# The modulated input of the QKV projection: full-precision value on ScalarE, traced with priority, low-part products last

## The chip, the core and the metric

One NeuronCore of one Trainium2 chip runs the whole program. The metric is the device time of one execution in microseconds; the kernel before took 1095.94 us (median of 3 runs, 1095.34 to 1098.32). Its engines, by the names of the profile: PE (TensorE matmul), PEld (its weight loads), DVE (VectorE), ACT (ScalarE), POOL (GpSimd), SP (the queue that issues the large loads). Each engine works through a queue of its own, in an order fixed when the program is built.

## The reference, cut to what matters

One layer of an encoder trunk: 256 tokens, width 2048, float32. The input is modulated by a scale and a shift that come from a conditioning vector, projected to queries, keys and values, and goes through attention, a projection, a layer norm, a modulated MLP and a second layer norm.

```
c_act = silu(c)
mod = c_act @ mod_w + mod_b                  # (2048,) @ (2048, 12288)
sh_m, sc_m, g_m, sh_f, sc_f, g_f = split(mod, 6)
hmix = x * (1 + sc_m) + sh_m                 # 256 x 2048
proj = hmix @ w_qkv + b_qkv                  # 2048 x 3072
...                                          # rotary positions, windowed attention with a sink
x = layer_norm(alpha * x + (1 + g_m) * (o @ w_o + b_o))
hff = x * (1 + sc_f) + sh_f
x = layer_norm(alpha * x + (1 + g_f) * (relu(hff @ w1 + b1)**2 @ w2 + b2))
```

## The kernel before

**Products in two parts.** Each operand of a large matmul is split into a rounded high part (type float32r) and a low part, the difference between the full value and the high part. A product is three matmuls on PE (function `mm3`): high input by high weight (L498), high input by low weight (L499), low input by high weight (L500). A weight tile `raw` (128 x 2048 floats, 1 MB) is loaded by SP (L202) and cut in two halves; for each half ACT writes the high part `wh` (L247) and DVE the low part `wl` (L218). There are five buffers of `wh` and five of `wl`, and eight of `raw` at first; a `raw` buffer is free again when both of its halves have been through L218, or when its other user is done.

**The modulation.** The input's 2048 features are 16 slices of 128. They are handled in six groups, g = 0 to 5, of 1, 1, 2, 4, 4 and 4 slices. For each group the scale and shift are themselves a product of the conditioning vector with 2 MB to 8 MB of weights (`in_modm`), done from the same `raw` buffers: partly on PE (L307), partly on DVE (L343, L345), whose part PE adds in at the end (L307 reading `onesf`). ACT copies the sums to `mrow` (L361), PE transposes them (L377), DVE adds the bias (L383) and one (L384), which gives the columns `scm` and `shm`.

**The modulated input.** The function `modulated(g)` then makes, for each slice of 128 x 256, the high part `hh` on ACT (L519), the full value in place on DVE (L520), and the low part `hl` = full minus high on DVE (L521). Groups 0 to 2 and, by `tc.keep_in_program_order`, these three instructions of every group are held to the order in which they were written; other instructions are placed by the scheduler of the framework, by their place in the trace and its estimate of when they can run.

**The projection.** A weight tile of a group of four slices is one chunk: four slices by 512 of the 3072 columns, which is 24 matmuls of 128 x 512. The function `qkv(g, ch)` runs a chunk: for each pair of slices, for both halves of the tokens, the three matmuls of each slice. Group 3 has six chunks in a row; here they are called chunk 1 to 6 of group 3. Groups 4 and 5 have three chunks each in this stage; the rest of theirs comes between the attention's steps. Results collect in PSUM (five buffers `pa`, two to a chunk) and are added to SBUF by DVE (`evict`, L537), two instructions to a chunk. Chunk 6 of group 3 is not evicted: it goes on into the first chunk of group 4 in the same two buffers. A group's last chunk calls `modulated(g + 1)` in its middle.

**Around it.** SP issues a load as soon as a `raw` buffer is free, in a planned order in which the modulation's weights and the chunks alternate. A one-element square root on ACT (`warm`, L874) stands in the trace after the attention, before the first layer norm (L761).

Of the kernel before, what the change touches and what calls it, by code (L numbers as in the profile page):

```python
# [2 lines left out]

# [1 line left out]

# [6 lines left out]
F32 = mybir.dt.float32  # L12
F32R = mybir.dt.float32r
I32 = mybir.dt.int32
AF = mybir.ActivationFunctionType
OP = mybir.AluOpType
# [4 lines left out]
S = 256  # L21
NT = S // 128
# [26 lines left out]
def hybrid_kernel(ctx: ExitStack, tc: tile.TileContext, a, out: bass.AP):  # L49
    nc = tc.nc  # L50
    cst = ctx.enter_context(tc.tile_pool(name="cst", bufs=1))
    sml = ctx.enter_context(tc.tile_pool(name="sml", bufs=4))
# [15 lines left out]
    def g4b(dt=F32):  # L68
        if not more:
            early.close()  # L70
            more.append(ctx.enter_context(tc.tile_pool(name="gen2", bufs=2 * MORE)))
        return more[0].tile([128, 1024], dt, tag="g4b", name="g4b")

    def g4(dt=F32):
        return gen.tile([128, 1024], dt, tag="g4", name="g4")

    def f32(x):
        return x.bitcast(F32)
# [5 lines left out]
    modmb, modfb, lnT = (pack[:, 80 + 32 * n:112 + 32 * n].rearrange("p (n k) -> p n k", n=2) for n in range(3))  # L84
# [8 lines left out]
    eps = cst.tile([128, 1], F32, name="eps")  # L93
# [73 lines left out]
    def bias_all(src, b):  # L167

        for h in range(2):
            nc.gpsimd.dma_start(b[h], src[:, h * 1024:h * 1024 + 1024].partition_broadcast(128))  # L170
        return lambda c: b[c // 2][:, (c % 2) * 512:(c % 2) * 512 + 512]
# [108 lines left out]
    S = Stream()  # L280
# [84 lines left out]
    def columns(m, mb, dst, k0, nk):  # L365

        r = m.r
        pt = pst.tile([128, 512], F32, name="pt")
        if m.pairs:
            nc.tensor.matmul(pt[:, :2], r[:, :128], both, start=True, stop=True)  # L370
            nc.vector.scalar_tensor_tensor(dst[0][:, k0:k0 + 1], pt[:, 0:1], 1.0, mb[:, 0, k0:k0 + 1],
                                           op0=OP.add, op1=OP.add)
            nc.vector.tensor_add(dst[1][:, k0:k0 + 1], pt[:, 1:2], mb[:, 1, k0:k0 + 1])
            return
        nh = m.w // 128
        for h in range(nh):
            nc.tensor.transpose(pt[:, h * 128:(h + 1) * 128], r[:, h * 128:(h + 1) * 128], ident)  # L377
        v = pt[:, :nh * 128].rearrange("p (h j q) -> p j h q", h=nh, j=4)[:, :, :, 0]
        cols = slice(k0, k0 + nk)
        for n in range(2):  # L380
            d = dst[n][:, cols].rearrange("p (j h) -> p j h", j=2)
            b = mb[:, n, cols].rearrange("p (j h) -> p j h", j=2)
            nc.vector.tensor_tensor(d, v[:, 2 * n:2 * n + 2], b, op=OP.add)  # L383
        nc.vector.tensor_scalar_add(dst[0][:, cols], dst[0][:, cols], 1.0)  # L384
# [28 lines left out]
    scm = cst.tile([128, NK], F32, name="scm")  # L413
    shm = cst.tile([128, NK], F32, name="shm")
# [77 lines left out]
    acc, xts, held, xs = {}, {}, {}, [None] * 4  # L492
# [4 lines left out]
    def mm3(ps, xh, xl, wh, wl, start, stop):  # L497
        nc.tensor.matmul(ps, xh, wh, start=start, stop=False)  # L498
        nc.tensor.matmul(ps, xh, wl, start=False, stop=False)  # L499
        S.prev = nc.tensor.matmul(ps, xl, wh, start=False, stop=stop).ins  # L500
# [10 lines left out]

    def modulated(g):
        m, k0, nk = m_mix[g]
        columns(m, modmb, (scm, shm), k0, nk)
        hh, hl = g4(F32R), g4(F32R)
        for k in range(nk):
            s = slice(k * 256, k * 256 + 256)
            xt, sc, sh = xts.pop(k0 + k), scm[:, k0 + k:k0 + k + 1], shm[:, k0 + k:k0 + k + 1]
            tc.keep_in_program_order(nc.scalar.activation(hh[:, s], xt, AF.Identity, scale=sc, bias=sh))  # L519
            tc.keep_in_program_order(nc.vector.tensor_scalar(xt, xt, sc, sh, op0=OP.mult, op1=OP.add))  # L520
            tc.keep_in_program_order(nc.vector.tensor_sub(hl[:, s], xt, f32(hh[:, s])))  # L521
        held[g] = hh, hl

    half = {}
# [1 line left out]
    def evict(c, pss):  # L526

        new = c not in acc
        if new:
            acc[c] = g4()  # L530
        for t in range(NT):
            av = acc[c][:, t * 512:t * 512 + 512]
            if new:
                bq(pss[t], c)
                nc.scalar.copy(av, pss[t])
            else:
                nc.vector.tensor_add(av, av, pss[t])  # L537

    def banks():
        return [psa.tile([128, 512], F32, name="pa") for _ in range(NT)]  # L540
# [22 lines left out]
    def qkv(g, ch):  # L563

        _, k0, nk = m_mix[g]
        hh, hl = held[g]
        wh, wl = S.main()
        per = 4 // nk
        for ci in range(per):
            p = ch * per + ci  # L570
            c = CORD[p]
            go_on, held_back = c in half, ((g, ch), p) in CARRY
            pss = half.pop(c, None) or banks()
            for k2 in range(0, nk, 2):
                for t in range(NT):
                    for k in (k2, k2 + 1):
                        s = slice(k * 256 + t * 128, k * 256 + t * 128 + 128)
                        mm3(pss[t], hh[:, s], hl[:, s], wh(ci * nk + k), wl(ci * nk + k),
                            k == 0 and not go_on, k == nk - 1 and not held_back)
                S.done()  # L580
                if per == 1 and k2 == 0:
                    yield
            if held_back:
                half[c] = pss
            else:
                evict(c, pss)
            if per == 2 and ci == 0:
                yield

    def run(gen, mid=()):  # L590
        next(gen)
        for f in mid:
            f()
        for _ in gen:
            pass
# [63 lines left out]
    def pairs_T(src, n):  # L659

        out = g4()
        for pr in range(n // 2):
            pt = pst.tile([128, 512], F32, name="pt")
            for i in range(2):
                for t in range(NT):
                    x = t * 512 + (pr * 2 + i) * 128
                    nc.tensor.transpose(pt[:, i * 256 + t * 128:i * 256 + t * 128 + 128], src[:, x:x + 128], ident)
            nc.scalar.copy(out[:, pr * 512:pr * 512 + 512], pt)
        return out
# [100 lines left out]
    sc = []  # L770
# [53 lines left out]
    def mids(n):  # L824
        out = []
        if 0 < n <= 16:
            out.append(lambda: probs_T(n - 1))
        if n < 16:
            out.append(lambda: normalise(n))
        return out  # L830
# [3 lines left out]
    for n in range(21):  # L834
        j, i = n // 4, n % 4
        if n < 16:
            scores(n)
        for f in todo:
            f()
        todo = []  # L840
        if n == 1:
            S.deep = False
        if n == 5:
            assert all(h is raws for h in S.home[S.at:]), "an early buffer is still in use"
        if n + 1 < len(LATE):
            w = qkv(*LATE[n + 1])
        else:
            if n == 5:
                ys, bo = [g4b() for _ in range(4)], bias_all(a["bo"], [g4b(), g4b()])
            w = project((n - 5) // 4, (n - 5) % 4)  # L850
        mid = mids(n)
        if j < 3:
            if i == 0:
                turn = rope(j + 1, 1)
            if 0 < i < 3 or n and i == 0:
                mid.append(lambda: qA.__setitem__(j + 1, next(turn)))
            if i == 3:
                mid.append(lambda: qT.__setitem__(j + 1, pairs_T(qA[j + 1], 4)))
        run(w, mid)
        if n == 0:  # L860
            next(turn)
        if 0 < n <= 16 and n % 2 == 0:
            todo.append(values(n - 1))
        if n == 9:

            for c in range(4):
                xs[c] = g4()
                i = nc.gpsimd.dma_start(xs[c].rearrange("p (t n) -> p t n", t=NT), a["x"][:, :, 512 * c:512 * c + 512])
                tc.add_manual_dep(i.ins, S.prev.name, AFTER, reason="not sooner")
        if n == 12:  # L870
            g1 = gate(m_gm)
        if n == 16:
            warm = sml.tile([128, 1], F32, name="warm")
            nc.scalar.activation(warm, eps, AF.Sqrt)  # L874
            st = [sml.tile([128, 4, 6], F32, name=f"st{t}", bufs=2) for t in range(NT)]


# [77 lines left out]
    for n, (kg, fq) in enumerate(W1A):  # L955
# [3 lines left out]
        wh, wl = S.main()  # L959
        for fp in range(2):  # L960
# [3 lines left out]
            for fi in range(2):  # L964
                o = ps[:, fi * 256:fi * 256 + 256]
                for k in range(4):
                    w = (fp * 2 + fi) * 4 + k
                    hb = ff_in(4 * kg + k)
                    hh, hl = hb[:, :256], hb[:, 256:]
# [91 lines left out]
    for c in range(3):  # L1061
        pss = ff_out(blk, us, c)
# [6 lines left out]
    for t in range(NT):  # L1069
# [5 lines left out]
        for c in (1, 0, 2, 3):  # L1075
            z = part(xs, t, c)
            g, b = (gb[n][c // 2][:, (c % 2) * 512:(c % 2) * 512 + 512] for n in range(2))
# [98 lines left out]
```

## Time and profile before

| | |
|---|---|
| Runs of the kernel before | 1095.34, 1095.94, 1098.32 us |
| The profiled execution: its own time | 1100.0 us |
| Its span, first to last instruction | 1098.2 us |
| PE busy | 1067.6 us (97%) |
| DVE busy | 804.2 us (73%) |
| ACT busy | 522.0 us (48%) |
| Mean granted TensorE clock | 0.991 |

The profile counts an engine as busy while an instruction of its runs; PE's ends are modelled, so neighbouring matmuls overlap in the records. Idle time is put down to what ended it. Times inside the execution are counted in microseconds from the first instruction. The stage that the change touches lies between about 37 and 145 us.

### The profile page before, as it was taken

What the parts mean: (1) busy time and instruction counts of PE and PEld (TensorE: products, weight loads), DVE (VectorE), ACT (ScalarE), POOL (GpSimd) and SP (SyncE); (2) the same over time, 40 slices, a digit from 0 to 9 for tenths busy, and PEclk for the clock granted to TensorE, in tenths of its full rate; (3) what the DMA queues carried; (4) which work ended last, traced back from release to release, by engine and by line L of the source; (5) the groups of instructions that cost most, each with busy time, mean ns of one, the idle gap of its engine ahead of it and who ended that gap; (6) DMA issues with size and microseconds to landing.
All of it is one profiled execution on the core that took longest, in us unless ns stands there. A gap on an engine that the chain in (4) does not pass through costs nothing.

```text
span 1098.2 us, 15487 instructions
## 1 busy us (share of the span) xinstructions
PE 1067.6 (97%) x6098; PEld 863.1 (79%) x6098; DVE 804.2 (73%) x1162; ACT 522.0 (48%) x806; POOL 30.0 (3%) x54
## 2 busy tenths in 40 slices
PE   8889999998999999999999999999999999999995
PEld 6657677665677799988888888888888888888884
DVE  4597899978899877754588889756666557665676
ACT  5333346765673537643344543344453334544340
POOL 1000000001000000000000010001000000000001
PEclk9989999999999999999999999999999999999998
DMA  9999987789985996555578788866555555557511
GB/s 384 425 427 425 427 357 280 271 297 379 377 315 201 361 360 244 185 192 192 195 301 303 272 313 306 312 220 225 184 189 190 197 196 186 178 185 267 191 75 77
DMA packets 43337, 292.70 MB, mean 267 GB/s; under 512 B 5104, under 2 KB 5232, under 8 KB 9472
## 3 DMA queue, kind: packets, MB, share of 16 engines
q1 hardware_dynamic: 39312, 279.85, 66.9%
q0 software_dynamic: 3200, 10.50, 2.7%
q10 hardware_dynamic: 752, 1.35, 0.3%
q8 instruction: 48, 0.79, 0.3%
q14 instruction: 25, 0.20, 0.0%
HBM read 289.57 MB, written 2.11 MB: 266 GB/s over the span
## 4 chain that ended last, share of the span: by engine, by line
PE 86%; DVE 7%; DMA 4%; ACT 2%; issue 1%; DVEq 0%; ACTq 0%
PE pa L995 16%; PE pa L500 15%; PE pa L498 15%; PE pa L499 15%; PE pa L996 8%; PE pa L972 3%; PE pa L971 3%; PE pa L973 3%; PE pm L307 3%; DVE wl L218 2%; DMA raw<-in_modm 2%; DMA raw<-in_modf 1%; DVE g L345 1%; DMA raw<-in_wqkv 1%; PE pa L687 1%; PE pa L743 1%
## 5 line engine op out<-in xcount | busy, mean ns | idle before, releaser
L218 DVE TENSOR_TENSOR wl<-raw,wh 128x1024 fp32r<-128x1024 f32 x332 | 403.9, 1223 | 223.6 <-ACT wh L247 222.9
L247 ACT CAST wh<-raw 128x1024 fp32r<-128x1024 f32 x332 | 347.1, 1051 | 441.3 <-PE pa L500 228.6
L498 PE MATMUL pa<-wh,g 128*128 128x512 f32 x816 | 324.1, 398 | 5.1 <-ACT g L519 2.6
L500 PE MATMUL pa<-wh,g 128*128 128x512 f32 x816 | 318.9, 392 | 4.1 <-DVE g L521 3.0
L499 PE MATMUL pa<-wl,g 128*128 128x512 f32 x816 | 320.0, 392 | 0.0
L995 PE MATMUL pa<-g,wh 128*128 128x512 f32 x768 | 270.1, 397 | 0.0
L996 PE MATMUL pa<-g,wl 128*128 128x256 f32 x768 | 214.9, 280 | 0.0
L498 PEld LDWEIGHTS pa<-wh,g 128*128 128x128 f32 x816 | 153.9, 189 | 46.8 <-issue 7.5
L500 PEld LDWEIGHTS pa<-wh,g 128*128 128x128 f32 x816 | 153.5, 188 | 41.2 <-DVE g L521 6.0
L499 PEld LDWEIGHTS pa<-wl,g 128*128 128x128 f32 x816 | 153.9, 189 | 33.0 <-issue 2.4
L995 PEld LDWEIGHTS pa<-g,wh 128*128 128x128 f32 x768 | 144.2, 188 | 36.0 <-issue 0.8
L996 PEld LDWEIGHTS pa<-g,wl 128*128 128x128 f32 x768 | 144.8, 189 | 0.1
L345 DVE SCALAR_TENSOR_TENSOR g<-raw,cact,g 128x1024 f32<-128x1024 f32 x65 | 82.6, 1280 | 2.8 <-DMA raw<-in_modf 2.3
L972 PE MATMUL pa<-g,wh 128*128 128x256 f32 x256 | 72.7, 285 | 0.4 <-DVE g L915 0.4
L971 PE MATMUL pa<-g,wh 128*128 128x256 f32 x256 | 72.5, 286 | 0.0
L973 PE MATMUL pa<-g,wl 128*128 128x256 f32 x256 | 72.3, 283 | 0.0
L307 PE MATMUL pm<-raw,cact 128*32 128x256 f32 (+2 forms) x776 | 48.8, 375 | 5.9 <-DMA raw<-in_modf 3.2
L971 PEld LDWEIGHTS pa<-g,wh 128*128 128x128 f32 x256 | 48.8, 192 | 1.3 <-issue 0.8
L972 PEld LDWEIGHTS pa<-g,wh 128*128 128x128 f32 x256 | 49.1, 192 | 0.9 <-DVE g L915 0.8
L973 PEld LDWEIGHTS pa<-g,wl 128*128 128x128 f32 x256 | 49.1, 192 | 0.0
L345 DVE SCALAR_TENSOR_TENSOR g4b<-raw,cact,g4b 128x1024 f32<-128x1024 f32 x32 | 40.7, 1280 | 9.0 <-DMA raw<-in_modgf 8.8
L307 PEld LDWEIGHTS pm<-raw,cact 128*32 128x32 f32 x776 | 20.9, 112 | 25.9 <-issue 11.5
(165 smaller groups left out, 741.6 us busy)
## 6 DMA issues: line engine op xcount, KB each, us to landing
raw<-in_w SPq DMA_DIRECT2D x64, 1024.0 KB, 4.9
raw<-in_w1b SPq DMA_DIRECT2D x48, 1024.0 KB, 5.0
raw<-in_modm SPq DMA_DIRECT2D x32, 1024.0 KB, 14.8
raw<-in_modf SPq DMA_DIRECT2D x32, 1024.0 KB, 6.9
raw<-in_wqkv SPq DMA_DIRECT2D x24, 1024.0 KB, 12.8
raw<-in_modgm SPq DMA_DIRECT2D x16, 1024.0 KB, 7.5
raw<-in_wo SPq DMA_DIRECT2D x16, 1024.0 KB, 7.5
raw<-in_w1a SPq DMA_DIRECT2D x16, 1024.0 KB, 7.6
```

The source lines that it names most:

```text
L218: self.pinned(nc.vector.tensor_sub(l, r, f32(self.hs[n])))
L247: self.pinned(nc.scalar.copy(h, s))
L307: i = nc.tensor.matmul(self.ps[32 * j:32 * j + 32, :w], lhsT[j] if type(lhsT) is list else lhsT, rhs[j], start=self.first, stop=stop)
L345: nc.vector.scalar_tensor_tensor(p[:, :e], s, cact[:, kt:kt + 1], p[:, :e], op0=OP.mult, op1=OP.add)
L498: nc.tensor.matmul(ps, xh, wh, start=start, stop=False)
L499: nc.tensor.matmul(ps, xh, wl, start=False, stop=False)
L500: S.prev = nc.tensor.matmul(ps, xl, wh, start=False, stop=stop).ins
L971: nc.tensor.matmul(o, wh(w, 128), hh, start=new, stop=False)
L972: nc.tensor.matmul(o, wh(w, 128), hl, start=False, stop=False)
L973: nc.tensor.matmul(o, wl(w, 128), hh, start=False, stop=end)
L995: nc.tensor.matmul(ps, wh(k, 128), hb, start=k == 0, stop=False)
L996: nc.tensor.matmul(ps[:, :256], wl(k, 128), hb[:, :256], start=False, stop=k == NK - 1)
```

## The change

The high-part and full-precision instructions of `modulated` are both on ACT for groups 1 to 5 (group 0 keeps DVE). From group 3 on the whole of `modulated`, its call of `columns` (the transposes L377 and the additions L383 and L384) included, is traced under `tc.high_priority()`, and its instructions are no longer held to program order among the rest; for groups 0 to 2 they are held as before. In `qkv`, of each pair of slices the eight products with the high part of the input come first and the four with the low part last. The one-element square root `warm` is gone.

```diff
     def modulated(g):
         m, k0, nk = m_mix[g]
-        columns(m, modmb, (scm, shm), k0, nk)
-        hh, hl = g4(F32R), g4(F32R)
-        for k in range(nk):
-            s = slice(k * 256, k * 256 + 256)
-            xt, sc, sh = xts.pop(k0 + k), scm[:, k0 + k:k0 + k + 1], shm[:, k0 + k:k0 + k + 1]
-            tc.keep_in_program_order(nc.scalar.activation(hh[:, s], xt, AF.Identity, scale=sc, bias=sh))
-            tc.keep_in_program_order(nc.vector.tensor_scalar(xt, xt, sc, sh, op0=OP.mult, op1=OP.add))
-            tc.keep_in_program_order(nc.vector.tensor_sub(hl[:, s], xt, f32(hh[:, s])))
+
+        with nullcontext() if S.pin else tc.high_priority():
+            columns(m, modmb, (scm, shm), k0, nk)
+            hh, hl = g4(F32R), g4(F32R)
+            for k in range(nk):
+                s = slice(k * 256, k * 256 + 256)
+                xt, sc, sh = xts.pop(k0 + k), scm[:, k0 + k:k0 + k + 1], shm[:, k0 + k:k0 + k + 1]
+                S.pinned(nc.scalar.activation(hh[:, s], xt, AF.Identity, scale=sc, bias=sh))
+                if g:
+                    S.pinned(nc.scalar.activation(xt, xt, AF.Identity, scale=sc, bias=sh))
+                else:
+                    S.pinned(nc.vector.tensor_scalar(xt, xt, sc, sh, op0=OP.mult, op1=OP.add))
+                S.pinned(nc.vector.tensor_sub(hl[:, s], xt, f32(hh[:, s])))
         held[g] = hh, hl
...
             for k2 in range(0, nk, 2):
-                for t in range(NT):
-                    for k in (k2, k2 + 1):
-                        s = slice(k * 256 + t * 128, k * 256 + t * 128 + 128)
-                        mm3(pss[t], hh[:, s], hl[:, s], wh(ci * nk + k), wl(ci * nk + k),
-                            k == 0 and not go_on, k == nk - 1 and not held_back)
+
+                for x in range(2):
+                    for t in range(NT):
+                        for k in (k2, k2 + 1):
+                            s = slice(k * 256 + t * 128, k * 256 + t * 128 + 128)
+                            w = ci * nk + k
+                            if x == 0:
+                                nc.tensor.matmul(pss[t], hh[:, s], wh(w), start=k == 0 and not go_on, stop=False)
+                                nc.tensor.matmul(pss[t], hh[:, s], wl(w), start=False, stop=False)
+                            else:
+                                S.prev = nc.tensor.matmul(pss[t], hl[:, s], wh(w), start=False,
+                                                          stop=k == nk - 1 and not held_back).ins
                 S.done()
...
         if n == 16:
-            warm = sml.tile([128, 1], F32, name="warm")
-            nc.scalar.activation(warm, eps, AF.Sqrt)
             st = [sml.tile([128, 4, 6], F32, name=f"st{t}", bufs=2) for t in range(NT)]
```

In the changed kernel the high-part activation is L521, the full-precision one L523 on ACT (L525 on DVE for group 0), the low part L526, the three matmuls of `qkv` L587, L588 and L590, and the eviction L542.

More of the change, by code (lines that the diff above doesn't have):

```diff
@@ L1 @@
 import math
-from contextlib import ExitStack
+from contextlib import ExitStack, nullcontext
 import numpy as np
```

## The prediction

> **What bounds the kernel now.** First the page: the span, the share of PE, its granted clock and the DMA in forty slices of 27.5 us.
>
> ```profile
> span 1098.2 us, 15487 instructions
> PE 1067.6 (97%) x6098; PEld 863.1 (79%) x6098; DVE 804.2 (73%) x1162; ACT 522.0 (48%) x806; POOL 30.0 (3%) x54
> ...
> PEclk9989999999999999999999999999999999999998
> DMA  9999987789985996555578788866555555557511
> ```
>
> PE is the bound. The projection's stage is different: there the DMA engines are full until about 130 us, and the clock dips in slice 3. All that the change touches lies in that stage, so I read it closely: first the waits of PE over the whole execution, then windows of it.
>
> ```profile
> PE pa L500 <- DVE g L521: 3.0, 3, 2.2
> PE pa L498 <- ACT g L519: 2.6, 2, 2.4
> ```
>
> ```profile
> 71.56:74.98 3.42, 1.50 (x12) 0.67 (x4) 2.81 (x3) 2.08 (x3) 0.95 (x1) 1.00 1.02 431
> 74.98:81.80 6.82, 6.35 (x26) 3.88 (x27) 6.64 (x12) 2.94 (x5) 0.00 (x0) 0.50 1.01 425
> ...
> 119.35:122.76 3.41, 1.73 (x19) 0.67 (x18) 3.41 (x4) 0.00 (x0) 0.00 (x0) 1.00 1.02 430
> ```
>
> Columns: window, length, busy time of PE, PEld, DVE, ACT, POOL, then clock, DMA share, GB/s. PE waits 5.6 us in total for modulated input, 2.4 and 2.2 us of it in one piece each. After the first, the clock is half for 6.82 us, which costs another 3.4 us of work; after the second it stays at 1.00. The timeline shows why PE waits.
>
> ```profile
> 72.90 1.99 ACT L247 CAST wh<-raw 128x1024 fp32r<-128x1024 f32 x2 [5.19 <-DMA raw<-in_wqkv]
> 74.80 2.07 ACT L519 ACTIVATE g<-g,shm,scm 128x256 fp32r<-128x256 f32 x4
> 75.45 0.79 PE L498 MATMUL pa<-wh,g 128*128 128x512 f32 x1 [2.39 <-ACT g L519]
> ```
>
> ```profile
> 120.12 1.28 DVE L345 SCALAR_TENSOR_TENSOR g<-raw,cact,g 128x1024 f32<-128x1024 f32 x1
> 121.31 0.41 DVE L520 TENSOR_SCALAR g<-g,scm,shm 128x256 f32<-128x256 f32 x1
> 121.64 1.28 DVE L345 SCALAR_TENSOR_TENSOR g<-raw,cact,g 128x1024 f32<-128x1024 f32 x1
> 122.83 0.42 DVE L521 TENSOR_TENSOR g<-g,g 128x256 fp32r<-128x256 f32 x1
> 123.31 0.50 PE L500 MATMUL pa<-wh,g 128*128 128x512 f32 x1 [2.23 <-DVE g L521]
> ```
>
> At group 3's entry ACT had two weight conversions, waiting for a DMA, queued ahead of the modulation. At group 4's entry DVE had work queued ahead of the low parts. The change aims at both.
>
> **What it removes.** The built order of the changed queues says what is now behind what; the rows say what each step costs. In group 3 the activations stand ahead of those conversions, and their columns ahead of two evictions. But PE does not arrive earlier for nothing: the first product of the next buffer (`pa_743`) now stands ahead of L307, and waits for an eviction.
>
> ```profile
> 66.34 1.28 DVE L537 TENSOR_TENSOR g<-g,pa 128x512 f32<-128x512 f32 x2
> ...
> 83.32 0.39 PE L499 MATMUL pa<-wl,g 128*128 128x512 f32 x1
> 83.55 0.39 PE L500 MATMUL pa<-wh,g 128*128 128x512 f32 x1
> ...
> 103.70 1.07 PE L307 MATMUL pm<-raw,cact 128*32 128x256 f32 x16
> 104.59 0.61 PE L307 MATMUL pm<-g,onesf 128*32 128x256 f32 x8
> 105.27 0.37 ACT L361 COPY mrow<-pm 128x256 f32<-128x256 f32 x1 [9.48 <-PE pm L307]
> ...
> 112.53 0.38 PE L377 MATMUL pt<-ident,mrow 128*128 128x128 f32 x2
> ```
>
> That eviction ran at 66.34, 0.68 us long. Two L520 leave the full DVE queue before it, 0.33 us each (121.31 to 121.64 above), so it ends near 66.4. From there PE has 18 matmuls at 0.227 us (83.32 to 83.55), three L307 blocks (0.9 from 103.70 to 104.59, 0.5 for the one with `onesf`, 1.0) and two transposes (0.2, as they overlap): 6.7 us, so group 3 begins near 73.2 instead of 75.45. Its activations are done before. Gain **2.2**; the half clock after the wait goes too, **3.4**. At group 4 the low parts stand ahead of three L345 and are ready in time: **2.4** with the restart. The last of the three L500 waits, at group 5, is part of the 0.8 us left of their 3.0: **0.3**. Together **8.3 us**.
>
> **What it adds at chunk borders.** With the low parts off DVE earlier, the built order puts the eviction of a chunk ahead of the next chunk's low weights. For chunk 3 of group 3:
>
> ```
> DVE: L542 pa_868, L542 pa_869, L218 wl_830, L218 wl_862    (chunk 2 out, then weights of chunk 3)
> PE:  ... L590 pa_868 x2, L590 pa_869 x2 | L587, L587, L588 <- wl_830
> ```
>
> Before, L218 `wl_830` had only the eviction of chunk 1 ahead of it, long since due:
>
> ```profile
> 83.97 0.69 DVE L537 TENSOR_TENSOR g<-g,pa 128x512 f32<-128x512 f32 x1 [1.97 <-PE pa L500]
> ...
> 84.58 2.36 DVE L218 TENSOR_TENSOR wl<-raw,wh 128x1024 fp32r<-128x1024 f32 x2
> ```
>
> An eviction starts 0.42 us after its last matmul starts (83.55 above), and holds DVE 0.61 us; L218 is usable 1.22 + 0.05 us after its start. Let T be the moment when the chunk's last matmul has gone. The first buffer's last matmul started at T - 0.68, so the evictions start at T - 0.26 and T + 0.35, L218 at T + 0.96, and PE may read the low weights at T + 2.2; it has two matmuls (0.45) until then. Stall **1.8 us**. The same order stands at chunk 4 (**1.8**); at chunk 5 only one eviction is ahead (**1.2**). Chunk 6 has none.
>
> From group 4's first to its second chunk the queue is eviction, L345, eviction, L218. An L345 holds DVE 1.19 us (120.12 to 121.31): T - 0.26 + 0.61 + 1.19 + 0.61 + 1.27 = T + 3.4, less 0.45: **3.0 us**. At the end of that second chunk PE needs the sum of the last L345, which is queued as eviction, L345, eviction, L345: T + 3.4, less the L307 block before it (0.9): **2.5 us**. Together **10.3 us**.
>
> **What it adds at group 5's entry.** Here the built order reads
>
> ```
> ACT: L361 mrow, L521, L521, L523, L523, L521, L521, L523, L523, L247 wh_1154, L247 wh_1172
> PE:  L307 onesf, L377, L377 | L587 <- wh_1154, ...      (third chunk of group 4)
> ```
>
> Before, L247 came straight after L361, and PE had sixteen matmuls between. Now PE has nothing: the weights it needs for group 4 are converted behind eight activations for group 5, and those wait for the transposes.
>
> ```profile
> 105.54 1.05 ACT L247 CAST wh<-raw 128x1024 fp32r<-128x1024 f32 x1
> ...
> 112.94 0.16 DVE L383 TENSOR_TENSOR scm<-pt,pack 128x4 f32<-128x4 f32 x1
> ...
> 113.14 0.17 DVE L384 TENSOR_SCALAR scm<-scm 128x4 f32<-128x4 f32 x1
> ```
>
> From the end of L307 (105.20): 0.07 to L361, 0.37 for it, 0.05 and 0.38 for L377, 0.03 and 0.37 for L383 to L384, then eight activations. Four took 2.07 us (74.80 above), so 0.49 each, 3.95. The full-precision ones do not stand in the trace on ACT; the same form with another output type does, and I take its price (0.6 each, the end of one, would add 0.4; I see no way below L519's). Then 0.05 + 1.05 for L247: **6.4 us** of stall, and 0.8 until L218 (1.22, less two matmuls) has the low half: **7.2 us**.
>
> **The clock.** PE was 1.50 us busy of 3.42 (44%) when the clock dropped for the two windows after it, and 1.73 of 3.41 (51%) when it did not. The stalls of 1.8 and less leave even a window that holds one whole busy for 1.8 of 3.41 us, 53% (a record of 0.39 us outlasts its pitch by 0.16): I take no loss. Those of 3.0 and 6.4 us do not; the one of 2.5 runs into the latter. I take one half-speed window of work each, 1.7 us: **3.4**; bounds are none (if the windows cut the stall in two) and two for each, 6.8.
>
> On this the page "TensorE: Matmul & The Clock Gate" of the Trainium skill, section "HAM oscillation — how this bites in real kernels", gives the rule that PE-idle gaps must be longer than about 3.4 us to throttle. The trace disagrees: a gap of 2.39 us did. By the rule only the 6.4 us stall would count, and my sum would be 1.7 us lower.
>
> **What costs nothing.** `warm` did not stand where it was written.
>
> ```profile
> 4.36 1.28 ACT L874 ACT_TABLE_LOAD   x1
> ...
> 11.32 0.27 ACT L361 COPY mrow<-pm 128x128 f32<-128x128 f32 x1 [3.28 <-PE pm L307]
> ```
>
> Its table load ran at 4.36, far from the norm, and a second one followed it; both lie ahead of 3.28 us in which ACT waited for PE. The square root's own load (L761) is there before and after. The longer ACT queue elsewhere is covered, as ACT is 48% busy. SP's order is the same; weights are freed later by up to 6 us, but PE is later too.
>
> **The sum.** 10.3 + 7.2 + 3.4 - 8.3 = **12.6 us**, say 12. After 145 us the queues are nearly the same and PE is the bound to the end, so a delay stays. The profiled execution took 1100.0 us for its span of 1098.2; the runs' median is 4 us lower, and a difference carries over: 1095.94 + 12 = **1108 us**.
>
> **The rivals.** *It does what it says*: the removed waits stay removed, because DVE and ACT are further ahead than I think and the borders hide. The 8.3 us are then the gain, less what the full DMA (share 1.01 to 1.02 in the windows) holds back: 1088 to 1091. It decides if the low weights do not pass through the queue behind evictions; the built order says that they do. Chance 0.08. *It cancels*: the borders cost, but the wait at group 5 shrinks, because PE comes late enough that its columns are done: 8.3 against about 9, 1093 to 1099. Against it: PE itself feeds those columns, immediately before, so lateness cannot help. Chance 0.06. *Slower, by the entry of group 5 alone*: if the borders are half hidden (5 of 10.3) and one window is lost, 7.2 + 5 + 1.7 - 8.3 = 5.6, 1101.5. This lies in the forecast's range.
>
> **How the numbers follow.** Forecast 0.86, rivals 0.08 and 0.06. The forecast's own bounds: no clock loss and half the borders give about +4, two windows each +16. The range leaves out most of the two rivals and the lowest end: 1100 to 1113. A change under 0.3% (3.3 us) cannot be told from none in this kernel: faster 0.08, same 0.06, slower 0.86.
>
> **What would show it.** Right: in the changed trace PE waits about 6 us in one piece for L247 near 137 to 144 us, behind eight activations on ACT; waits of 1 to 3 us for L218 at the chunk borders between 84 and 126; half clock after 126 or 143; no wait for the modulated input at 73. Wrong: low weights that are ready at the borders, or L247 done while PE still has work.

## The result, and the profile after

The changed kernel took 1111.10 us (median of 4 runs, 1109.46 to 1112.58); the kernel before took 1096.62 us in the runs beside it (4 runs, 1095.34 to 1098.32). The ratio is 1.0131, 95% interval 1.0109 to 1.0152: 14.5 us slower. The profiled execution took 1111.63 us. First the page: span, busy times, granted clock and DMA in forty slices.

```profile
span 1109.9 us, 15475 instructions
PE 1069.4 (96%) x6098; PEld 863.4 (78%) x6098; DVE 798.4 (72%) x1147; ACT 528.2 (48%) x818; POOL 30.0 (3%) x54
...
PEclk9999979999999999999999999999999999999998
DMA  9999977688996797555578888776555555557522
```

PE's busy time grew by 1.8 us only, the span by 11.7: the rest is waiting. The clock dips in slice 6 (139 to 166 us), and DMA has more slack in slices 6 to 9 than before (7768 against 8778). The view of what PE waited for (total, times, longest) names it:

```profile
PE pa L588 <- DVE wl L218: 7.0, 4, 2.8
PE pa L587 <- ACT wh L247: 5.5, 1, 5.5
...
PE pm L307 <- DVE g L345: 2.3, 1, 2.3
PE pa L587 <- DVE g L542: 2.1, 3, 1.2
```

The waits for modulated input are gone at groups 3 to 5. In their place stand four waits for low weights, one for high weights and one for the sum of L345. The timeline at the border between chunks 2 and 3 of group 3, the first border with a wait, DVE and then PE:

```profile
86.43 1.28 DVE L542 TENSOR_TENSOR g<-g,pa 128x512 f32<-128x512 f32 x2 [2.89 <-PE pa L590]
87.64 2.36 DVE L218 TENSOR_TENSOR wl<-raw,wh 128x1024 fp32r<-128x1024 f32 x2
...
86.69 0.61 PE L587 MATMUL pa<-wh,g 128*128 128x512 f32 x2
88.91 0.50 PE L588 MATMUL pa<-wl,g 128*128 128x512 f32 x1 [1.61 <-DVE wl L218]
```

DVE had been idle for 2.89 us when it waited, at the head of its queue, for chunk 2 to end; the conversion behind it, which chunk 3 needs, could have run in that time. In the kernel before it ran at 84.58, during chunk 2. At group 5's entry the same happens on ACT:

```profile
140.65 0.37 ACT L361 COPY mrow<-pm 128x256 f32<-128x256 f32 x1 [23.68 <-PE pm L307]
142.20 1.10 ACT L521 ACTIVATE g<-g,shm,scm 128x256 fp32r<-128x256 f32 x2 [1.18 <-DVE scm L384]
...
145.67 0.59 ACT L523 ACTIVATE g<-g,shm,scm 128x256 f32<-128x256 f32 x1
146.16 3.87 ACT L247 CAST wh<-raw 128x1024 fp32r<-128x1024 f32 x4
...
141.07 0.69 PE L377 MATMUL pt<-ident,mrow 128*128 128x128 f32 x2 [0.49 <-ACT mrow L361]
147.25 1.22 PE L587 MATMUL pa<-wh,g 128*128 128x512 f32 x2 [5.49 <-ACT wh L247]
```

ACT was idle for 23.68 us, then did eight activations, and only then the conversion for which PE stood still. The windows (start and end, length, busy time of PE, PEld, DVE, ACT, POOL, then clock, DMA share, GB/s) show what that did to the clock:

```profile
125.76:129.17 3.41, 1.13 (x5) 0.94 (x6) 3.41 (x5) 0.00 (x0) 0.00 (x0) 1.00 0.61 195
129.17:132.58 3.41, 3.41 (x10) 2.64 (x9) 2.43 (x2) 0.00 (x0) 0.00 (x0) 0.50 1.01 423
...
139.41:142.82 3.41, 1.77 (x10) 0.49 (x10) 0.40 (x4) 0.99 (x3) 0.00 (x0) 0.50 0.66 202
...
149.64:153.06 3.42, 3.42 (x10) 2.65 (x9) 3.35 (x3) 1.35 (x2) 0.00 (x0) 0.50 0.67 230
```

One half-speed window after the border at 128 us, four from 139.41 to 153.06. From 147.25 on PE worked in 5.8 us of those four, so 2.9 us were lost there and 1.7 in the first.

### The profile page after: what moved, and what is told of

Its sections match the earlier page's. It is cut to its first block, busy times and chain, and to the rows that moved or that the text cites. A ratio compares the mean times of both kernels' runs of the same rounds, so it can differ in the third digit from the quotient of the medians.

```text
span 1109.9 us, 15475 instructions
## 1 busy us (share of the span) xinstructions
PE 1069.4 (96%) x6098; PEld 863.4 (78%) x6098; DVE 798.4 (72%) x1147; ACT 528.2 (48%) x818; POOL 30.0 (3%) x54
## 4 chain that ended last, share of the span: by engine, by line
PE 84%; DVE 8%; DMA 5%; issue 2%; ACT 2%; DVEq 0%; SPq 0%; ACTq 0%
PE pa L1005 16%; PE pa L498 12%; PE pa L499 12%; PE pa L500 12%; PE pa L1006 8%; PE pa L588 3%; PE pa L982 3%; PE pa L981 3%; PE pa L983 3%; PE pa L587 3%; PE pa L590 3%; PE pm L307 2%; DMA raw<-in_modm 2%; DVE wl L218 2%; DVE g L345 2%
## 5 line engine op out<-in xcount | busy, mean ns | idle before, releaser
L218 DVE TENSOR_TENSOR wl<-raw,wh 128x1024 fp32r<-128x1024 f32 x332 | 403.8, 1224 | 224.3 <-ACT wh L247 223.7
L247 ACT CAST wh<-raw 128x1024 fp32r<-128x1024 f32 x332 | 348.0, 1054 | 431.1 <-PE pa L500 202.1
L498 PE MATMUL pa<-wh,g 128*128 128x512 f32 x648 | 255.4, 394 | 2.7 <-ACT g L540 1.8
L500 PE MATMUL pa<-wh,g 128*128 128x512 f32 x648 | 252.3, 390 | 0.0
L498 PEld LDWEIGHTS pa<-wh,g 128*128 128x128 f32 x648 | 121.6, 188 | 33.2 <-issue 3.5
L500 PEld LDWEIGHTS pa<-wh,g 128*128 128x128 f32 x648 | 121.6, 188 | 25.5
L499 PEld LDWEIGHTS pa<-wl,g 128*128 128x128 f32 x648 | 121.7, 188 | 24.9 <-issue 0.8
L345 DVE SCALAR_TENSOR_TENSOR g<-raw,cact,g 128x1024 f32<-128x1024 f32 x65 | 83.0, 1284 | 0.5
L587 PE MATMUL pa<-wh,g 128*128 128x512 f32 x168 | 68.0, 413 | 7.6 <-ACT wh L247 5.5
L588 PE MATMUL pa<-wl,g 128*128 128x512 f32 x168 | 67.0, 407 | 7.0 <-DVE wl L218 7.0
```

The costliest lines, as they stand in the source:

```text
L218: self.pinned(nc.vector.tensor_sub(l, r, f32(self.hs[n])))
L247: self.pinned(nc.scalar.copy(h, s))
L345: nc.vector.scalar_tensor_tensor(p[:, :e], s, cact[:, kt:kt + 1], p[:, :e], op0=OP.mult, op1=OP.add)
L587: nc.tensor.matmul(pss[t], hh[:, s], wh(w), start=k == 0 and not go_on, stop=False)
```

## The experiments

In what follows "the 960th matmul" is counted from PE's first as number 0; all versions but one have the same 6098, so the start of the same number in two traces shows how far one is ahead. A "miss" is a time outside the range that was expected.

**The kernel before, once more** (`before_again`), without any edit.

> The kernel before once more, unchanged, for a second profile. Theory that the half clock of 74.98 to 81.80 us in the first profile (3.4 us of work) is an accident of that execution: the wait of about 2.4 us for L519 near 75 us stands again but the clock after it is 1.00, mean clock 0.994 or more, time 1094 to 1097. Rival, the wait always brings the half clock: clock 0.991, time 1098 to 1100.

It took 1095.49 us, 4.5 us less than the first profiled execution. The wait at group 3's entry is there, and after it the clock is full:

```profile
75.17 0.51 PE L498 MATMUL pa<-wh,g 128*128 128x512 f32 x1 [2.06 <-ACT g L519]
```

```profile
70.18:73.59 3.41, 2.93 (x24) 1.43 (x22) 3.25 (x7) 0.96 (x2) 0.59 (x1) 1.00 1.02 430
73.59:77.00 3.41, 1.83 (x19) 0.88 (x19) 3.26 (x5) 3.01 (x6) 0.36 (x1) 1.00 1.00 423
```

The granted clock changes only at edges that lie a multiple of 3.413 us apart (in the changed kernel's trace, for example, at 26.769 and 30.182), and their phase differs from run to run. Here an edge cut the wait in two, and neither window was less than 54% busy. In the first profile one window held 1.9 of the 2.4 us. So the half clock at 75 us, 3.4 us of work, is not in every execution: of the 71 runs of before that stood beside the versions, 51 have a granted clock of 0.994 or more, and 6 the 0.991 of the first profile. This profile is the fairer base: the changed kernel's own time is 16.1 us above it.

**One part of the change at a time, on the kernel before.** The products' order alone (`hl_last`), the move to ACT alone (`act_alone`), priority without held order alone (`priority_alone`); the edits in short:

```
hl_last:         for x in range(2): for t: for k:   # high input first, low input last
act_alone:       if g: keep_in_program_order(nc.scalar.activation(xt, xt, ...))   # was on DVE
priority_alone:  with nullcontext() if S.pin else tc.high_priority():  # and S.pinned(...) for keep_in_program_order(...)
```

> The kernel before with one part of the change alone: of each pair of slices the low-part products come last. Modulated input, its order and the small square root are as before. Everything computed is the same. Queue-order theory: the built DVE and ACT queues are those of before, with the evictions behind the next chunk's low weights, so no wait comes at the borders; group 4's wait for its low parts shrinks from 2.4 us to about 1, since eight products instead of two precede the first that needs one: 1094 to 1097. Rival, product order: the border waits come from finishing both buffers of a chunk within 0.9 us of each other: 1101 to 1107.

> The kernel before with one part of the change alone: the full-precision value of groups 1 to 5 is on ACT, in the written order (high, full, high, full), held as before; products and small square root as before. Everything computed is the same. Queue-order theory: the evictions stand where they stood, so no border waits; the second, third and fourth high parts stand behind one to three activations of 0.49 us more, so the waits at the entries of groups 3 and 4 grow by 0.5 to 1 each: 1096.5 to 1099. Rival, relief of DVE: sixteen instructions of 0.33 us less on DVE bring the low parts earlier: 1093 to 1095.5. Rival, the extra work on ACT is what makes the changed kernel slow: 1103 or more.

> The kernel before with one part of the change alone: from group 3 on the modulated input is no longer held to order and is traced with priority; the full-precision value stays on DVE, the products keep their old order, the small square root stays. Everything computed is the same. Theory that the borders come from no longer holding the order: in the built DVE queue both evictions stand ahead of the next chunk's low weights, as in the changed kernel; since the old product order ends the first buffer half a chunk earlier, only the second eviction is late, and each of four borders costs about 1.2 us instead of 1.8 to 3, the sum at group 5's entry 1.9; the entries of groups 3 and 4 save 4 to 5: 1097 to 1101, with waits for L218 of about 1.2 us. Rival, the move to ACT is what frees DVE for early evictions, so that no border waits here: 1092 to 1096. Rival, priority alone is the whole change: 1108 or more.

Products' order: 1095.57 us, ratio 0.9987 (0.9971 to 1.0003). ACT: 1097.15, ratio 1.0011 (0.9997 to 1.0024). Both are within their ranges, both intervals include no change, and neither kernel has a wait for L218 at a border. Priority without held order: 1102.62, ratio 1.0063 (1.0040 to 1.0086), a little above its range. Its PE waits:

```profile
PE pa L499 <- DVE wl L218: 6.3, 4, 1.9
...
PE pm L307 <- DVE g L345: 2.3, 1, 2.3
```

With neither the move to ACT nor the new order of products, the waits at the borders are there. Each took 1.6 to 2.1 us where 1.2 was expected. The timeline of the same border as above, DVE and PE:

```profile
85.74 0.69 DVE L539 TENSOR_TENSOR g<-g,pa 128x512 f32<-128x512 f32 x1 [0.67 <-PE pa L500]
86.34 2.35 DVE L218 TENSOR_TENSOR wl<-raw,wh 128x1024 fp32r<-128x1024 f32 x2
...
85.54 0.61 PE L498 MATMUL pa<-wh,g 128*128 128x512 f32 x2
87.61 0.50 PE L499 MATMUL pa<-wl,g 128*128 128x512 f32 x1 [1.46 <-DVE wl L218]
```

The second eviction starts 0.43 us after the chunk's last matmul does (85.31), later than the sum had it, and PE has only two matmuls before it needs the low weights.

**All but the loosened order** (`held_no_priority`): the changed kernel with `keep_in_program_order` for `S.pinned` and without the priority.

> The whole change except that the modulated input is held to its written order and has no priority, as in the kernel before: full-precision value on ACT for groups 1 to 5, low-part products last, no small square root. Everything computed is the same. Theory that no longer holding the order makes the borders: none of the waits for L218 at the borders and none for L247 at group 5's entry: 1095 to 1098, the time of the kernel before. Rival, ACT's work or the products' order: 1103 to 1110.

1098.28 us, ratio 1.0019 (1.0005 to 1.0032): 0.3 above its range and 2 us above before, no wait for L218 or L247. So of 14.5 us some 12 come only when the order is loosened or the priority given.

**Priority or loosened order?** (`no_priority`: `with nullcontext():` in place of the priority.)

> The changed kernel without the priority: the modulated input of groups 3 to 5 is neither held to order nor given priority. In the built queues the evictions still stand ahead of the next chunk's low weights; at group 5's entry one activation instead of eight stands ahead of the weights of group 4's third chunk. Everything computed is the same. Theory that the borders come from no longer holding the order, and only group 5's entry from the priority: the entry's wait for L247 shrinks by seven activations of 0.49 us, 3.4, and one half-speed window of 1.7 may go: 1106 to 1108, with the waits of 1.2 to 3 us for L218 still there. Rival, priority makes the borders: 1096 to 1100.

1109.29 us, ratio 1.0119 (1.0106 to 1.0132): a miss by 1 to 3 us, though the waits are as expected:

```profile
PE pa L588 <- DVE wl L218: 7.0, 4, 2.8
...
PE pa L587 <- ACT wh L247: 2.0, 1, 2.0
```

The waits at the borders are those of the changed kernel to 0.01 us: losing the held order makes them, not the priority. The wait for L247 shrank by 3.5 us, seven activations. The 960th matmul came at 166.24 instead of 172.26, but by the 1800th 2.7 us were left of these 6.0 (315.41 and 318.15).

**The evictions put back** (`evict_held`): the changed kernel, with the evictions held to order.

```diff
-                nc.vector.tensor_add(av, av, pss[t])
+                tc.keep_in_program_order(nc.vector.tensor_add(av, av, pss[t]))
```

> The changed kernel with one thing more: the two evictions of a chunk (the additions into SBUF on DVE) are held to the order in which they were written among the other held instructions, which puts each pair of low weights ahead of the eviction that stood before it. Everything computed is the same. Queue-order theory: the five waits at the chunk borders go (1.77, 1.75, 1.17, 2.97 and 2.57 us in the changed kernel's trace, 10.2 in all) and the half-speed window at 129 us with them (1.7 us of work): 1111.1 - 11.9 = 1099, between 1097 and 1102; the wait of 5 to 6 us for L247 at group 5's entry stays. Rival, product order: the waits come from finishing both buffers of a chunk at its end, so wherever the evictions stand PE waits: 1109 to 1113. Rival, transfers: the loads are the next thing late and take half of it back: 1104 to 1106.

1098.14 us, ratio 1.0008 (0.9994 to 1.0023): 13 us from two instructions per chunk. DVE at the same border:

```profile
82.32 2.35 DVE L218 TENSOR_TENSOR wl<-raw,wh 128x1024 fp32r<-128x1024 f32 x2
...
85.79 0.68 DVE L542 TENSOR_TENSOR g<-g,pa 128x512 f32<-128x512 f32 x1
```

Chunk 3 begins at 85.00 here; its low weights are made during chunk 2, and chunk 2's evictions come after them. PE keeps its wait at group 5's entry whole, and of the L218 rows only the 0.5 us behind that entry is left:

```profile
PE pa L587 <- ACT wh L247: 5.5, 1, 5.5
...
PE pa L588 <- DVE wl L218: 0.5, 1, 0.5
```

**Group 5 put back** (`g5_held`): the changed kernel, with group 5's modulated input held and without priority. **Both put back** (`both_held`), with group 5's full-precision value on DVE. The lines shown are those of `g5_held`; `both_held` has the line of `evict_held` besides, and `if 0 < g < 5:` for `if g:`.

```diff
+        hold = tc.keep_in_program_order if g < 3 or g == 5 else S.pinned
-        with nullcontext() if S.pin else tc.high_priority():
+        with nullcontext() if S.pin or g == 5 else tc.high_priority():
...
-                S.pinned(nc.scalar.activation(hh[:, s], xt, AF.Identity, scale=sc, bias=sh))
+                hold(nc.scalar.activation(hh[:, s], xt, AF.Identity, scale=sc, bias=sh))
```

> The changed kernel, but for group 5 the modulated input is traced without priority and held to the order in which it was written, so that ACT converts the weights of group 4's third chunk straight after L361 and the eight activations stand behind four more conversions. Everything computed is the same. Queue-order theory: the waits at group 5's entry go (1.0 for L377 and 5.8 for L247) and with them most of the half clock after 139 us (2.9 us of work): 1111.1 - 9.7 = 1101.5, up to 1104 if the wait of 2.6 us before it still costs a half-speed window; the borders keep their 10.2 us. Rival, work on ACT: the eight extra microseconds of activations hold ACT up wherever they stand, and the next conversions are late by as much: 1108 to 1112. Rival, transfers: half comes back: 1106.

> Both of the above in one kernel: evictions held to their written order, group 5's modulated input without priority and held to its order, and for group 5 the full-precision value on DVE as in the kernel before. Groups 1 to 4 have it on ACT, with priority for 3 and 4, and the low-part products stay last. Everything computed is the same. Queue-order theory: the two gains add: 1111.1 - 11.9 - 9.7 = 1089.5, between 1087 and 1093, which is faster than the kernel before by the removed waits at group 3's and group 4's entry (about 8 us). Rival, transfers: the stage is fed by DMA engines that are full to 130 us, so what is won at the entries comes back as waits for raw weights: 1095 to 1099. Rival, product order: 1101 or more.

Group 5 alone: 1109.37, ratio 1.0106 (1.0076 to 1.0136), a miss. The time lies in the range of the rival that ACT's work makes the next conversions late, but by another way. The entry is repaired; look further down PE's timeline:

```profile
139.78 0.73 PE L588 MATMUL pa<-wh,g 128*128 128x512 f32 x2 [0.51 <-ACT wh L247]
...
266.47 0.50 PE L500 MATMUL pa<-wh,g 128*128 128x512 f32 x1 [1.28 <-DVE g L759]
...
270.30 1.94 PE L307 MATMUL pm<-raw,cact 128*32 128x256 f32 x16 [2.20 <-DMA raw<-in_modf]
```

8.3 us ahead of the changed kernel at the 960th matmul, it is 2.9 ahead at the 1800th: waits for L759 and for a load, and a half-speed window from 270.2 to 273.6, take it back. Both: 1096.50, ratio 1.0007 (0.9992 to 1.0021), where 1089.5 was expected; the rival, transfers, had 1095 to 1099. Here are its ACT and PE at group 5's entry:

```profile
127.70 1.99 ACT L247 CAST wh<-raw 128x1024 fp32r<-128x1024 f32 x2 [0.48 <-DMA raw<-in_wqkv]
130.18 1.99 ACT L247 CAST wh<-raw 128x1024 fp32r<-128x1024 f32 x2 [0.48 <-DMA raw<-in_wqkv]
...
128.80 0.51 PE L588 MATMUL pa<-wh,g 128*128 128x512 f32 x1 [1.09 <-ACT wh L247]
```

Each pair of conversions waits for its megabyte. PE came to the 840th matmul 1.8 us ahead of the kernel before (125.73 and 127.53) and left the stage 0.4 us behind it (154.67 and 154.27 at the 960th). The waits cost clock too: in the window that holds them (127.67 to 131.08) PE was busy for 1.57 of 3.41 us, and the next one is at half speed, which costs 1.7 us of work.

**Group 3 alone** (`g3_only`): priority and ACT for group 3 only, its evictions held, groups 4 and 5 as before.

```diff
+        hold = tc.keep_in_program_order if g != 3 else S.pinned
+        with nullcontext() if g != 3 else tc.high_priority():
...
-                nc.vector.tensor_add(av, av, pss[t])
+                i = nc.vector.tensor_add(av, av, pss[t])
+                if g == 3:
+                    tc.keep_in_program_order(i)
```

> A version that keeps only what the traces so far show to help: for group 3 alone the modulated input is traced with priority and has its full-precision value on ACT, the evictions in group 3 are held to their written order, groups 4 and 5 are held and have that value on DVE as in the kernel before, and the low-part products stay last. Everything computed is the same. Queue-order theory: against the products' order alone (1095.6) the wait of 2.07 us for L519 at group 3's entry goes and nothing is put in its place at the borders: 1093 to 1094.5, so 2 to 3.5 us under the kernel before. Rival, transfers: the loads are as late as before and the gain comes back as waits for raw weights before 270 us: 1095 to 1097.

1096.62 us, ratio 1.0003 (0.9993 to 1.0014): the rival's time again. PE gains at group 3 and stands 4.64 us at group 4's entry, behind two conversions that wait for a load:

```profile
115.02 1.99 ACT L247 CAST wh<-raw 128x1024 fp32r<-128x1024 f32 x2 [10.33 <-DMA raw<-in_wqkv]
116.91 2.07 ACT L522 ACTIVATE g<-g,shm,scm 128x256 fp32r<-128x256 f32 x4
...
117.56 0.80 PE L590 MATMUL pa<-wh,g 128*128 128x512 f32 x1 [4.64 <-ACT g L522]
```

Two half-speed windows follow (116.25 to 123.08). The load sets the start of this pair of conversions, whatever PE has won before: 113.10, 113.13 and 113.32 in `before_again`, `hl_last` and `act_alone`, 115.01, 115.02 and 115.28 in `order_no_warm` (below), `g3_only` and `both_held`. The first three have the small square root `warm`, the last three lack it, so by these rows some 1.9 of the 4.64 us belong to its absence.

**The clock by itself** (`fill`): sixteen products of ones after L377, in group 5's wait.

```diff
             columns(m, modmb, (scm, shm), k0, nk)
+            if g == 5:
+                pf = pst.tile([128, 512], F32, name="pt")
+                for _ in range(16):
+                    nc.tensor.matmul(pf, onesr, onesr[:, None, :].to_broadcast([128, 4, 128]), start=True, stop=True)
```

> The changed kernel with sixteen more products of ones (128 x 512, their result is not used) on PE after the transposes L377 at group 5's entry, where PE waits 5.8 us for L247. They take 3.6 us at full clock and end before the weights come, so that no wait is taken away: only the clock can change. Everything else computed is the same. Theory that the wait costs clock as well as time: the half-speed stretch after the wait (139.41 to 153.06 us) ends by 143 us, 2.9 us of work is won: 1107 to 1109, granted clock 0.990 instead of 0.987. Rival, the clock does not follow the share of busy time: 1110 to 1113.

1112.32 us, ratio 1.0152 (1.0135 to 1.0169): a miss, in the range of the rival that the clock does not follow the share of busy time. Yet the clock did recover (mean 0.993 in this profile; four half-speed windows became one, 148.4 to 151.8). Counted without the sixteen, the kernel was only 1.3 us ahead by the 960th matmul and level again by the 2200th, after a wait of 2.49 us for a load near 375. In this profile, what the clock gave, a load took.

**The small square root** (`order_no_warm`): the products' order alone, and without `warm`.

```diff
-            warm = sml.tile([128, 1], F32, name="warm")
-            nc.scalar.activation(warm, eps, AF.Sqrt)
```

> The kernel before with the low-part products last and without the small square root; nothing else is changed, and the result is the same. The products' order alone gave 1095.57 against 1096.6 before, not yet told from no change. Theory that the small square root costs nothing and the order of products saves about 1 us at the entry of group 4: 1095 to 1096, ratio 0.998 to 1.000. Rival, its two table loads on ACT hold something up: 1093 to 1094.5.

1097.79 us, ratio 1.0019 (1.0005 to 1.0034), slower than the same kernel with `warm` (0.9987, 0.9971 to 1.0003); neither theory had that. The windows of the two, `hl_last` first, over a stretch in which DMA is full:

```profile
40.00:110.00 70.00, 66.48 (x387) 47.82 (x386) 59.91 (x78) 23.45 (x30) 1.91 (x2) 1.00 1.01 426
```

```profile
40.00:110.00 70.00, 65.95 (x376) 46.77 (x376) 57.81 (x73) 23.81 (x30) 1.90 (x2) 0.98 1.01 420
```

The same share, 1.4% fewer bytes. All five profiles with the square root show 426 GB/s there, all nine without it 420 or 421, whatever else they change. Over 128 us that is 1.8 us by which loads are late. Why, no run tells. Not all of the 2 us need be that: the profile without `warm` has two half-speed windows (77.09 to 80.50 and 124.87 to 128.29) that `hl_last` has not, and over all runs its granted clock is lower (0.9923 against 0.9938).

## Why the prediction was right, and where it was not

**The borders: right to a tenth.** Forecast 1.8, 1.8, 1.2, 3.0, 2.5, together 10.3. The excess over the matmuls' pitch in the changed trace is 1.77, 1.75, 1.17, 2.97 and 2.57, together 10.2. `evict_held` shows the cause: one order put back, 13 us gone. One reading was loose: the eviction of chunk 1 was not "long since due", its row shows DVE waiting 1.97 us for it; what counts is that it was a chunk older than the weights needed.

**Group 5's entry: right.** Forecast 6.4 + 0.8 (the steps given add up to 6.3); measured 1.01 for L377, 5.80 for L247 and 0.44 for L218, 7.25 in all. `no_priority` shows the cause: seven activations fewer, 3.5 us less wait. The price of one full-precision activation on ACT was taken from L519's, and held: the eight took 3.96 us (142.20 to 146.16) where 3.95 was forecast.

**Group 3's entry: mis-sized.** Forecast 2.2 from a start near 73.2 (66.4 and 6.7 make 73.1). The wait is gone, but group 3 began at 74.55, 0.6 before the 75.17 of `before_again`: the eviction that was to end near 66.4 let PE go at 67.22, after waits for L542 of 0.86, 0.40 and 1.38 us (0.65 and 0.37 in `before_again`), and the way from there took 7.33 us where 6.7 was summed.

**The half clock removed (3.4): this step failed.** It was real in the profile shown and absent from the run that is nearer the median. The sum was made on 1100.0, with the half clock in it; "a difference carries over" then took it from a median that did not hold it. The sum fits the profile it was made on (1100.0 + 12 = 1112 against 1111.63) and is short on the medians, 1108 against 1111.1, by about those 3.4 us. That 44% busy drops the clock and 51% does not is only roughly so: in the fourteen profiles every full-speed window with less than 45% was followed by a half-speed one and none with more than 58%, but between these both occur. 1.96 of 3.42 us (`held_no_priority`, 73.67) dropped it, 1.54 of 3.41 us (`no_priority`, 270.07) did not. And where the window's edge falls is chance. In `no_priority` a border wait of 2.97 us, the changed kernel's to a hundredth, was cut in two and dropped nothing:

```profile
123.35:126.76 3.41, 1.79 (x8) 1.12 (x6) 2.49 (x4) 0.00 (x0) 0.00 (x0) 1.00 0.75 310
126.76:130.18 3.42, 2.24 (x10) 1.83 (x11) 3.42 (x3) 0.00 (x0) 0.00 (x0) 1.00 0.85 302
```

The page "TensorE: Matmul & The Clock Gate" of the Trainium skill, section "Part 1: The HAM clock gate", says that the window is free-running, 4096 cycles long, and that its phase differs by run. The traces agree, at 3.413 us.

**The clock added:** forecast 3.4, lost in that profile 1.7 + 2.9 = 4.6. The granted clock of all runs points the same way: 0.9885 mean over the changed kernel's 4, 0.9939 over the 71 runs of before that stood beside the versions.

**The sum of what was measured, against the fairer base:** 10.2 + 7.25 + 4.6, less 0.6 at group 3 and the 3.3 us that `before_again` waits at the entries of groups 4 and 5 (1.01 + 0.33 + 1.60 + 0.40), is 18.1; the 960th matmul is 18.0 later (172.26 and 154.27). So the total came near partly by luck: against this base the forecast missed 3.4 (half clock), 1.6 (group 3) and 1.2 us (clock added), and 0.6 us (groups 4 and 5, 2.7 forecast) and the 1.9 us of the next paragraph stood against them.

**"A delay stays": failed by 1.9 us.** At the 1800th matmul 16.1 of 18.0 are left. The kernel before itself waits there for loads (2.00 us at 258.58 in `before_again`, 0.92 in the changed kernel at 274.67), and a late PE waits less; that is 1.1 of the 1.9 us. In `g5_held` and `no_priority` too, later waits took back more than half of what was won.

**"`warm` costs nothing" (to leave it out): failed**, by about 2 us where loads are the bound, a part of which may be clock. In the changed kernel itself little of it shows, since DMA has slack behind the stalls (share 0.61 in the window at 125.76).

**The rival "it does what it says"** rested on 8.3 us to be won. `both_held` has no wait at the entries of groups 3 and 4 and none at a border, `g3_only` none at group 3's entry, and both end level with before: 3.4 of the 8.3 us were not in the median run, and the loads, which come no sooner, and the clock after the waits for them took the rest. The prediction mentioned the full DMA beside this rival and priced it too low. Both versions also lack `warm`, without which that load comes 1.9 us later; with it kept they were not run, so whether they would then beat before is open. The one version below before, the products' order alone, has an interval that includes no change.

## What to carry to other kernels

An instruction that waits for the very work that PE is doing now must not stand ahead of a conversion that PE needs next: the added cost is the queue from the end of that work to the conversion's end, and it can be summed from the built order and single rows to a tenth of a microsecond. A gain does not add up like that: before counting a removed wait, look at what else is full in that stage (here DMA at a share of 1.01) and ask when the next load lands. Ask also whether the profiled execution is the median one: a half clock in its windows may be that run's own.

## What the hardware did that was not expected

The same wait, to a hundredth of a microsecond, cost a half-speed window in one run and none in another. Without one square root of a single element at the start, and so without two ACT table loads of 1.28 us there, loads ran at 420 instead of 426 GB/s through the whole full stretch. Only in the pair `hl_last` and `order_no_warm` does nothing else change; in all fourteen profiles the rate goes with the square root. The mechanism is open.
